# Two up matrices side by side on TensorE's column halves in the 64-slot expert steps of a two-layer mixture-of-experts block

## The chip, the cores and the metric

One core of one Trainium2 chip runs the whole program. The metric is device time in microseconds (us), the median of several runs. The engines are PE (TensorE matmul), ACT (ScalarE), DVE (VectorE), POOL (GpSimd) and SP (SyncE, which issues most transfers).

## What is computed

A block of two layers over 256 tokens of width 1024 (with 256 context tokens beside them in the first layer). Each layer has a group of sequence mixers and then a mixture of 16 experts, of which each token takes two. All inputs are float32. Cut to the part that the change touches:

```python
def moe(h, w_router, b_router, w1, w3, w2):
    logits = (h @ w_router).astype(F32) + b_router.astype(F32)
    ...
    for e in range(N_EXPERTS):
        he = jax.nn.silu(h @ w1[e]) * (h @ w3[e])
        out = out + gate[..., e:e + 1].astype(h.dtype) * (he @ w2[e])
    return out

def reference(x, c, ctx, ...):
    for l in range(DEPTH):
        ...
        x = x + gt2 * moe(h2, router_w, router_b, moe_w1[l], moe_w3[l], moe_w2[l])
    return rms_norm(x, final_norm_g)
```

`w1[e]` and `w3[e]` (the up matrices) are 1024 x 512, `w2[e]` (the down matrix) is 512 x 1024.

## The kernel before

Tokens are sorted to experts: each expert `e` of layer `l` has `SLOT[l][e]` slots (rows of tokens), and what doesn't fit runs in a loop of extra passes between experts 1 and 2 (`extras`). `moe` (L1923) walks the experts; each is a generator, `expert32` (L2163) or `expert`, whose stages are interleaved with those of the expert before, so that the up products of `e` stand around the down product of `e - 1`. In layer 1 all experts run in `expert32`, fourteen of them with 64 slots, one with 128 (e = 4) and one with 96 (e = 8). In layer 0 only the seven with 64 slots do; the others split each weight into a high and a low part for three matmuls. These 21 steps with 64 slots are the subject.

A step's weights are six loads of 1 MB ("raw"): j = 0, 1 are the two row halves of w1 (four blocks of 128 rows each), j = 2, 3 those of w3, j = 4, 5 the two column halves of w2. The table `USE` (L43) sets the order in which they are fetched: (e,0), then the down halves of e - 1, then (e,1), (e,2), (e,3). SP issues them into a ring of buffers, 10 in layer 0 and 12 in layer 1, at most three under way at once (`FLIGHT`); a load waits until PE has read the ring's buffer.

`expert32` with 64 slots (G = 2) uses half of PE's columns for one matmul, because the stationary operand has 64 columns. `tile_position` gives even row blocks the lower and odd row blocks the upper half of the columns:

```python
            a = k % G
            kw = dict(tile_position=(0, a * m)) if G > 1 else {}
            ... nc.tensor.matmul(ps[a * m:a * m + m], lhsT=lhsT, rhs=next(ws), start=k < G, stop=k >= n - G, ...)
```

A product therefore leaves as two partial sums, in partitions 0 to 63 and 64 to 127 of a PSUM bank, to be joined:

- Up: `p1` (w1) and `p3` (w3) are two banks of sixteen matmuls together. ACT copies `p1` and DVE copies `p3` to SBUF (tiles `al`). Eight matmuls against the constant `fold`, two identity blocks stacked, add the halves and transpose at once. ACT's Silu and a DVE product make `h` (tile `ah`), which is the stationary operand of the down product.
- Down: for each of the two column halves four matmuls into a bank; ACT copies the upper partitions (tile `s`), DVE adds the lower ones, and ACT scales by the gate (ACTIVATE, `y` or `yf`). When both halves are done, POOL issues a scatter with addition of 64 rows of 4 KB into the accumulator `ybd` in HBM (`add_rows`, L2153).
- The last expert (e = 15) is not scattered. `combine` joins its rows to the accumulated ones through a one-hot matrix on PE, after `ybd` has been read back by SP and multiplied on POOL.

PE, ACT, DVE, POOL and SP each run their instructions in order. A scheduler fixes each order at build time. Two stages that recur below: `xg` is the gathered token rows of an expert, transposed on PE (`tp`) and copied by ACT (`ah`); `sc`, `mm` and `tp` are the names of PSUM banks for up products, down products and transposes. In the profile nearly every operation carries one line number, L385 (L395 in the changed program), that of a recording helper, so its rows are read by these names.

Of the kernel before, what the change touches and what calls it, by code (L numbers as in the profile page):

```python
# [19 lines left out]
P = 128  # L20
# [20 lines left out]

STAT = 2
USE = [(0, j) for j in range(4)]  # L43
for _e in range(1, NE):
    _p = [(_e, 0), (_e - 1, 4), (_e - 1, 5)]
    USE += (_p if _e != STAT else _p[1:] + _p[:1]) + [(_e, j) for j in range(1, 4)]
USE += [(NE - 1, 4), (NE - 1, 5)]
# [19 lines left out]
TILE = [np.cumsum([0] + [-(-n // P) for n in SLOT[l]]).tolist() for l in range(L)]  # L67
NXMAX = 16
# [323 lines left out]
class Kern:  # L392
# [114 lines left out]
    def pump(self):  # L507
        I = self.I
        while self.lp < len(self.items):
# [9 lines left out]
            if k[0] == "x" and k[2] < BUFS[f"R{k[1]}"]["raw2"]:  # L519
                src = I["wmoe"][self.wpos(k[1], *USE[k[2]])]  # L520
                t = self.rp.tile([P, 2048], F32, tag="raw2", name=self.nm("raw"), bufs=BUFS[f"R{k[1]}"]["raw2"])
            else:
# [3 lines left out]
                src = {"x": lambda: I["wmoe"][self.wpos(k[1], *USE[k[2]])], "w": lambda: I["win"][k[1], k[2]], "o": lambda: I["wout"][k[1], k[2]],  # L526
# [102 lines left out]
    def setup(self):  # L629
# [17 lines left out]
        self.fold = cp.tile([P, HALF], F32, name="fold")  # L647
        nc.vector.tensor_tensor(self.fold, self.ident[:, 0:HALF], self.ident[:, HALF:P], op=ALU.add)
# [1058 lines left out]
    def route(self, l, NT):  # L1707
# [139 lines left out]
        nc.gpsimd.dma_start(tab, self.slv(l)[:, 0:TILE[l][NE]])  # L1847
        yield
# [17 lines left out]
    def first_slots(self, l):  # L1866
# [7 lines left out]
        for tag, n, dt in (("src", STAT, I32), ("cnt", 16, F32), ("key", 16, F32), ("cap", 16, F32), ("big", nd * nd, F32), ("rke", 16, F32),  # L1874
                           ("sel", nd * nd, BF16), ("ext", 16, F32), ("inc", 16, F32), ("exc", 16, F32), ("nx", 1, I32),
                           ("at", 16, F32), ("ov", 16 * NT, F32), ("u", 16 * NT, F32), ("w", 16 * NT, F32),
                           ("XT", 4 * NT, F32), ("q", 2 * NT, F32), ("r", 2 * NT, F32), ("ri", 2 * NT, I32), ("tab", 2 * TILE[l][NE], I32)):
# [45 lines left out]
    def moe(self, l, route):  # L1923
# [12 lines left out]
        def begin(e):  # L1936
            if self.whole(l, e):
                gens[e] = self.expert32(l, source(e), (xg.pop(e), *sl[e]), SLOT[l][e], last=e == NE - 1)
# [9 lines left out]
        for e in range(NE):  # L1948
            for n, t in zip(both(e), range(TILE[l][e], TILE[l][e + 1])):
                sl[n] = self.slot_of(self.rt["tab"][:, t])  # L1950
        begin(0)
        next(gens[0])
        for e in range(NE):
            if e == STAT:

                while len(self.pre) < AHEAD2[l]:
                    m, j = USE[self.wi]
# [15 lines left out]
            if e == NE - 1:  # L1973
                while self.wi < len(USE):
                    self.pre.append(self.fetch(source(USE[self.wi][0])(USE[self.wi][1])))
# [187 lines left out]
    def expert32(self, l, wsrc, tile, m, last=False):  # L2163
# [9 lines left out]
        G = 2 if m == HALF else 1  # L2173

        def weights():
            for j in range(6):
                raw = self.load(wsrc(j))
                for k in range(4):
                    yield raw[:, k * 512:(k + 1) * 512]

        ws = weights()

        def mm(ps, lhsT, k, n):
            a = k % G
            kw = dict(tile_position=(0, a * m)) if G > 1 else {}
            self.last_mm = nc.tensor.matmul(ps[a * m:a * m + m], lhsT=lhsT, rhs=next(ws), start=k < G, stop=k >= n - G,
                                            skip_group_check=True, **kw)
# [11 lines left out]
        p1, p3 = self.pssc(), self.pssc()  # L2199
        for w, ps in enumerate((p1, p3)):  # L2200
            for k in range(KB):
                mm(ps, x[k], k, KB)
                if (w, k) in ((0, 1), (0, 3), (1, 3)):
                    yield
        s1 = self.act("al", F32)
        if G > 1:
            s3 = self.act("al", F32)
            nc.scalar.copy(s1, p1)
            nc.vector.tensor_copy(s3, p3)
        else:  # L2210
            nc.scalar.activation(s1[:m], p1[:m], AF.Silu)
# [3 lines left out]
        if G > 1:  # L2215
            for j, s in enumerate((s1, s3)):
                for k in range(4):
                    o = (4 * j + k) * m
# [155 lines left out]
```

## Time and profile before

| | |
|---|---|
| median of 3 runs | 1288.04 us (1285.62 to 1288.15) |
| the profiled execution's own time | 1281.23 us |
| its span | 1279.6 us |
| PE busy | 1128.9 us, 88% |
| DVE, ACT, POOL busy | 722.7, 531.5, 162.9 us |
| mean granted clock of PE | 0.945 of full speed |

The span runs from the first to the last instruction of one execution on the core; the run's time lies 1.6 us above it. The profiled execution is 0.53% faster than the median. In the span the experts of layer 0 stand at about 444 to 710 us, those of layer 1 at 985 to 1257 us, with the loop of extra passes at 1014 to 1026 us; the rest is mixers, routing and the final norm.

### The profile page before, as it was taken

The page shows a single profiled execution, that of the slowest core. Times are in us where ns is not written, and L with a number is a line of the kernel's source. Part 1 is how long each engine was busy: PE and PEld are TensorE (multiplying, and loading weights), DVE is VectorE, ACT ScalarE, POOL GpSimd, SP SyncE. Part 2 cuts the span into 40 slices and gives each one's busy share as a digit, 9 for nine tenths or more (in the row PEclk, how much of TensorE's full clock was granted, in tenths as well). Part 3 has the DMA queues.
Part 4 walks back from the last instruction along what each step waited for, and adds up shares of the span by engine and source line. Part 5 has one row for each costly group of instructions (what it writes and reads, how often), then busy time and mean ns, then how long its engine had stood idle before and what let it go on. Part 6 is the DMA issues. An engine that isn't in the chain of part 4 may idle for free. (4 is left out here: it accounts for less than half of the span.)

```text
span 1279.6 us, 16887 instructions
## 1 busy us (share of the span) xinstructions
PE 1128.9 (88%) x5789; PEld 714.7 (56%) x5789; DVE 722.7 (56%) x1824; ACT 531.5 (42%) x877; POOL 162.9 (13%) x204
## 2 busy tenths in 40 slices
PE   4999999997977699999998799998893699998885
PEld 2677677765866467655444277684771344533332
DVE  6396579788588554455444659599975110101115
ACT  5232642675316554555434452563940212222222
POOL 0100200100004210211100100200202111111102
PEclk9999999997987899999999899999995999998997
DMA  8773753443917798899994744554468989999961
GB/s 304 255 250 113 257 206 112 168 176 125 393 67 276 252 341 321 310 367 380 387 394 163 283 180 143 177 203 162 147 234 320 372 333 390 376 391 389 412 248 67
DMA packets 62010, 334.06 MB, mean 261 GB/s; under 512 B 12217, under 2 KB 13657, under 8 KB 27104
## 3 DMA queue, kind: packets, MB, share of 16 engines
q1 hardware_dynamic: 51840, 313.44, 64.5%
q0 software_dynamic: 10080, 19.50, 5.9%
q8 instruction: 47, 0.77, 0.2%
q14 instruction: 43, 0.35, 0.1%
HBM read 317.51 MB, written 19.15 MB: 263 GB/s over the span
## 5 line engine op out<-in xcount | busy, mean ns | idle before, releaser
L385 DVE TENSOR_TENSOR lo<-raw,hi 128x1024 fp32r<-128x1024 f32 x172 | 206.6, 1220 | 90.2 <-ACT hi L385 78.1
L385 PE MATMUL sc<-raw,ah 128*64 128x512 f32 (+3 forms) x750 | 214.1, 628 | 14.8 <-SPq L2042 11.7
L385 ACT CAST hi<-raw 128x1024 fp32r<-128x1024 f32 x169 | 172.3, 1047 | 123.2 <-PE sc L385 58.2
L385 PEld LDWEIGHTS sc<-raw,ah 128*64 128x64 f32 (+3 forms) x750 | 63.0, 146 | 115.2 <-issue 100.6
L385 PE MATMUL mm<-hi,ah 128*128 128x512 f32 (+3 forms) x264 | 108.7, 413 | 5.0 <-ACT hi L385 4.6
L385 PE MATMUL mm<-lo,ah 128*128 128x512 f32 (+3 forms) x264 | 106.5, 403 | 1.8 <-DVE lo L385 1.6
L385 PE MATMUL mm<-hi,al 128*128 128x512 f32 (+3 forms) x264 | 105.4, 401 | 0.3 <-DVE al L385 0.3
L385 PE MATMUL mm<-raw,ah 128*64 128x512 f32 (+3 forms) x378 | 98.3, 592 | 2.5 <-DVE rel L385 1.9
L385 DVE COPY al<-sc 128x512 f32<-128x512 f32 x21 | 14.5, 691 | 149.3 <-PE sc L385 129.6
L385 PE MATMUL mm<-ah,hi 128*128 128x512 f32 (+1 forms) x224 | 86.9, 393 | 0.8 <-DVE ah L385 0.8
L385 PE MATMUL sc<-hi,ah 128*128 128x512 f32 (+3 forms) x176 | 74.2, 423 | 14.2 <-issue 10.5
L385 PE MATMUL mm<-ah,lo 128*128 128x512 f32 (+1 forms) x224 | 83.0, 371 | 0.9 <-DVE lo L385 0.9
L385 PE MATMUL mm<-al,hi 128*128 128x512 f32 (+1 forms) x224 | 82.9, 370 | 0.0
L385 PE MATMUL ad<-raw,cT 128*32 128x256 f32 (+1 forms) x512 | 67.3, 526 | 10.8 <-DMA raw<-in_wada_dram 9.1
L385 DVE TENSOR_TENSOR s<-s,mm 64x512 f32<-64x512 f32 (+1 forms) x43 | 29.2, 678 | 81.5 <-ACT s L385 81.5
L385 PE MATMUL sc<-lo,ah 128*128 128x512 f32 (+3 forms) x176 | 72.7, 413 | 1.7 <-DVE lo L385 1.6
L385 PE MATMUL sc<-hi,al 128*128 128x512 f32 (+3 forms) x176 | 72.1, 409 | 1.8 <-DVE al L385 1.8
L385 PEld LDWEIGHTS mm<-hi,ah 128*128 128x128 f32 (+3 forms) x264 | 49.2, 187 | 28.3 <-ACT hi L385 6.5
L385 PEld LDWEIGHTS mm<-raw,ah 128*64 128x64 f32 (+3 forms) x378 | 32.6, 142 | 57.7 <-issue 48.5
L385 PEld LDWEIGHTS tp<-fold,al 128*128 128x128 f32 x336 | 40.5, 191 | 38.6 <-ACT al L385 15.6
L385 PE MATMUL tp<-fold,al 128*128 128x64 f32 x336 | 43.8, 278 | 15.8 <-ACT al L385 8.6
L385 PEld LDWEIGHTS mm<-lo,ah 128*128 128x128 f32 (+3 forms) x264 | 49.4, 187 | 14.6 <-DVE lo L385 4.6
(433 smaller groups left out, 1952.8 us busy)
## 6 DMA issues: line engine op xcount, KB each, us to landing
raw<-in_wmoe_dram SPq DMA_DIRECT2D x192, 1024.0 KB, 7.9
raw<-in_wada_dram SPq DMA_DIRECT2D x32, 1024.0 KB, 5.1
raw<-in_win_dram SPq DMA_DIRECT2D x24, 1024.0 KB, 6.2
raw<-in_wad_dram SPq DMA_DIRECT2D x16, 1024.0 KB, 4.9
raw<-in_wout_dram SPq DMA_DIRECT2D x8, 1024.0 KB, 5.0
x<-in_tok_dram SPq DMA_DIRECT2D x8, 512.0 KB, 7.4
raw<-ybd SPq DMA_DIRECT2D x6, 512.0 KB, 4.7
slot<-yf SPq DMA_DIRECT2D x36, 64.0 KB, 2.8
```

What stands on the lines that cost most here:

```text
L385: r = f(*a, **k)
```

## The change

In a step with 64 slots the column halves now take different matrices, not different row blocks. For each of the eight row blocks two matmuls run with the same stationary operand: w1 on the lower, w3 on the upper half, into one bank. All rows of a product are summed in place, so nothing is left to be joined. One ACT copy brings the bank to SBUF, four plain transposes of 128x128 follow, and Silu and product read the two halves of each transposed block. The eight down matmuls likewise put the two column halves of w2 side by side in one bank, one ACTIVATE scales all 128 partitions, and the scatter writes 128 pieces of 2 KB (row and half) instead of 64 of 4 KB.

Raws are now read in pairs, (0,2) and (1,3), then (4,5); `USE` becomes a table for each layer, in which both raws of the first pair come before the down halves of e - 1. For the scatter's 128 rows and gates the routing adds a table `tab2` (two small loads on POOL's queue a layer) and `row2` (one POOL operation a layer). In the last expert the upper half of the down bank is copied by ACT and the lower is read in place. Steps with other numbers of slots keep their instructions. In layer 0's seven steps the four transposes stand behind other matmuls of the neighbouring expert in four cases, and right behind the step's own up matmuls in three. At the start of layer 1 and in its mixers a few small loads and weight matmuls move by some places.

```diff
+def _use(l):
+    out = []
+    for e in range(NE):
+        js = [0, 2, 1, 3] if SLOT[l][e] == HALF else [0, 1, 2, 3]
+        n = 2 if SLOT[l][e] == HALF else 1
+        down = [(e - 1, 4), (e - 1, 5)] if e else []
+        up = [(e, j) for j in js]
+        out += down + up if e == STAT else up[:n] + down + up[n:]
+    return out + [(NE - 1, 4), (NE - 1, 5)]
...
-        self.fold = cp.tile([P, HALF], F32, name="fold")
-        nc.vector.tensor_tensor(self.fold, self.ident[:, 0:HALF], self.ident[:, HALF:P], op=ALU.add)
+        self.half = cp.tile([P, 1], F32, name="half")
+        nc.vector.reduce_sum(self.half, self.ident[:, HALF:], axis=AX.X)
...
+        tab2 = self.rt["tab2"] = f([P, TILE[l][NE], 2], "tab2", I32)
+        for h in range(2):
+            nc.gpsimd.dma_start(tab2[h * HALF:(h + 1) * HALF], self.slv(l)[0:HALF, 0:TILE[l][NE]])
...
+            if e == 0:
+                nc.gpsimd.tensor_scalar(self.row2, self.rt["tab2"][:, :, 0], 2.0, self.half, op0=ALU.mult, op1=ALU.add)
...
+        if m == HALF:
+            self.nc.gpsimd.indirect_dma_start(out=self.ybd[l].rearrange("r (h c) -> (r h) c", h=2), out_offset=bass.IndirectOffsetOnAxis(ap=rows, axis=0),
+                                              in_=y[:, 0:512], in_offset=None, bounds_check=2 * self.rt["NT"] * P - 1, oob_is_err=False,
+                                              compute_op=ALU.add)
+            return
...
-        p1, p3 = self.pssc(), self.pssc()
-        for w, ps in enumerate((p1, p3)):
-            for k in range(KB):
-                mm(ps, x[k], k, KB)
-                if (w, k) in ((0, 1), (0, 3), (1, 3)):
-                    yield
...
         if G > 1:
-            s3 = self.act("al", F32)
-            nc.scalar.copy(s1, p1)
-            nc.vector.tensor_copy(s3, p3)
+            ps = self.pssc()
+            ws = chain.from_iterable(weights(c, 2 + c) for c in range(2))
+            for k in range(KB):
+                for a in range(2):
+                    mm(ps, x[k], next(ws), a, k == 0, k == KB - 1)
+                if k in (1, 3, 5):
+                    yield
+            nc.scalar.copy(s1, ps)
...
-            for j, s in enumerate((s1, s3)):
-                for k in range(4):
-                    o = (4 * j + k) * m
-                    nc.tensor.matmul(pt[:, o:o + m], lhsT=s[:, k * P:(k + 1) * P], rhs=self.fold, start=True, stop=True)
+            for k in range(4):
+                nc.tensor.transpose(pt[:, k * P:(k + 1) * P], s1[:, k * P:(k + 1) * P], self.ident)
...
+        if G > 1:
+            ps = self.psmm()
+            ws = weights(4, 5)
+            for k in range(4):
+                for a in range(2):
+                    mm(ps, h[:, k * m:(k + 1) * m], next(ws), a, k == 0, k == 3)
+            if not last:
+                nc.scalar.activation(y[:, 0:512], ps, AF.Copy, scale=half[1])
+                self.add_rows(l, y, half[0], m)
+                return
+            t = self.act("al", F32)[:m]
+            nc.scalar.copy(t, ps[m:2 * m])
```

The orders move at three places that matter below. First PE in a late step of layer 1, before: `ah_10268` feeds the down product of e - 1, `al_10347` and `al_10348` are the copies of `p1` and `p3`, `xg` belongs to e + 2.

```order
L385 MATMUL sc_10262<-raw_10264,ah_10247 64x512 x4
L385 MATMUL mm_10283<-raw_10284,ah_10268 64x512 x4
L385 MATMUL mm_10294<-raw_10295,ah_10268 64x512 x4
L385 MATMUL sc_10262<-raw_10308,ah_10247 64x512 x4
L385 MATMUL tp_10361<-fold,al_10347 128x64 x4
L385 MATMUL tp_10422<-cst,xg_8996 128x64 x4
L385 MATMUL sc_10263<-raw_10314,ah_10247 64x512 x4
L385 MATMUL tp_10422<-cst,xg_8996 128x64 x4
L385 MATMUL sc_10263<-raw_10341,ah_10247 64x512 x4
L385 MATMUL tp_10361<-fold,al_10348 128x64 x4
```

And the same place in the changed program, from the end of a step's up product on (`al_10205` is the one copy; the matmuls on `raw_2180` and `raw_2181` alternate, and the next expert's down matmuls on `raw_10303` and `raw_10305` do):

```order
L395 MATMUL sc_10206<-raw_10247,ah_10195 64x512
L395 MATMUL sc_10206<-raw_10245,ah_10195 64x512
L395 MATMUL sc_10206<-raw_10247,ah_10195 64x512
L395 MATMUL tp_10290<-cst,al_10205 128x128 x3
L395 MATMUL sc_10280<-raw_2180_10281,ah_10272 64x512
L395 MATMUL tp_10290<-cst,al_10205 128x128
L395 MATMUL tp_10337<-cst,xg_8903 128x64 x8
L395 MATMUL sc_10280<-raw_2181_10283,ah_10272 64x512
L395 MATMUL sc_10280<-raw_2180_10281,ah_10272 64x512
...
L395 MATMUL sc_10280<-raw_2181_10283,ah_10272 64x512
L395 MATMUL mm_10302<-raw_10303,ah_10289 64x512
L395 MATMUL mm_10302<-raw_10305,ah_10289 64x512
```

The two sets of folds, one ahead of the second and one behind the last up matmuls, have become one set of transposes behind the last up matmul, and one matmul of the next expert's up product has slipped in among them; the down matmuls keep their place among the up matmuls.

Second, ACT over such a step, before:

```order
L385 COPY s_2250_10474<-mm_10467 64x512
L385 ACTIVATE yf_6832<-s_2250_10474,rtab_9095 64x512
L385 COPY s_2253_10485<-mm_10478 64x512
L385 ACTIVATE yf_6832<-s_2253_10485,rtab_9095 64x512
L385 COPY al_10531<-sc_10446 128x512
L385 ACTIVATE al_10551<-tp_10542 128x256
L385 COPY ah_10612<-tp_10603 128x512
```

and changed:

```order
L395 ACTIVATE yf_6737<-mm_10228,rtab_1966_9004 128x512
L395 COPY al_10205<-sc_10206 128x512
L395 ACTIVATE al_10295<-tp_10290 128x256
L395 COPY ah_10346<-tp_10337 128x512
...
L395 ACTIVATE yf_6737<-mm_10376,rtab_1966_9004 128x512
L395 COPY al_10353<-sc_10354 128x512
```

Four operations on the down product ahead of the copy of the up bank have become one; the last two rows are the same pair a step later, with no transposed token rows (`ah`) left to copy.

Third, DVE at the end of the program, before:

```order
L385 COPY al_10696<-sc_10625 128x512
L385 TENSOR_TENSOR ah_10699<-al_10709,tp_10700 128x256
L385 TENSOR_SCALAR rel_10713<-rtab_9095 64x1 x2
L385 TENSOR_SCALAR ah_10712<-iota_b,rel_10713 64x128 x2
L385 TENSOR_TENSOR s_2307_10724<-s_2307_10724,mm_10719 64x512
L385 SCALAR_TENSOR_TENSOR s_2308_10727<-s_2307_10724,rtab_9095,raw_10688 64x512
L385 TENSOR_TENSOR raw_10718<-s_2308_10727,raw_10718 64x512
L385 TENSOR_TENSOR s_2310_10736<-s_2310_10736,mm_10731 64x512
L385 SCALAR_TENSOR_TENSOR s_2311_10739<-s_2310_10736,rtab_9095,raw_10688 64x512
L385 TENSOR_TENSOR raw_10718<-s_2311_10739,raw_10718 64x512
```

and changed:

```order
L395 TENSOR_TENSOR ah_10413<-al_10419,tp_10414 128x256
L395 TENSOR_SCALAR rel_10423<-rtab_9002 64x1 x2
L395 TENSOR_SCALAR ah_10422<-iota_b,rel_10423 64x128 x2
L395 SCALAR_TENSOR_TENSOR s_2215_10440<-mm_10429,rtab_9002,raw_10405 64x512
L395 SCALAR_TENSOR_TENSOR s_2216_10444<-al_10438,rtab_9002,raw_10405 64x512
L395 TENSOR_TENSOR raw_10428<-s_2215_10440,raw_10428 64x512
L395 TENSOR_TENSOR raw_10428<-s_2216_10444,raw_10428 64x512
```

The copy of `p3` and the two additions to `s` are gone, and the two halves of the last product stand side by side, not one after the other.

## Rows read from the trace of the kernel before

All times are us of the span. A row of a group of instructions names line, engine, operation, output<-input with tile shapes, and the count of records.

**Rows 1.** The page, part 1: busy us (share of span) and instructions.

```profile
PE 1128.9 (88%) x5789; PEld 714.7 (56%) x5789; DVE 722.7 (56%) x1824; ACT 531.5 (42%) x877; POOL 162.9 (13%) x204
```

**Rows 2.** Busy time by stretch, all engines, then granted clock, DMA share, GB/s.

```profile
core 0: us, PE busy (x) PEld busy (x) DVE busy (x) ACT busy (x) POOL busy (x), PEclk, DMA share, GB/s
...
1056.00:1106.00 50.00, 50.00 (x218) 23.12 (x216) 5.78 (x10) 11.82 (x20) 7.36 (x6) 1.00 1.01 383
...
1156.00:1206.00 50.00, 43.65 (x216) 17.65 (x214) 7.42 (x12) 11.83 (x21) 6.17 (x5) 0.93 1.01 399
1206.00:1257.00 51.00, 43.73 (x207) 17.16 (x204) 11.18 (x16) 11.46 (x20) 8.67 (x5) 0.93 0.64 255
1257.00:1279.60 22.60, 9.72 (x16) 3.76 (x16) 11.12 (x27) 5.83 (x13) 2.75 (x3) 0.68 0.13 47
```

**Rows 3.** Waits of 1026 to 1257 us: total us, times, longest.

```profile
PE tp L385 <- ACT al L385: 8.6, 7, 1.3
...
PE tp L385 <- DVE al L385: 5.6, 7, 0.8
...
PEld sc L385 <- DMA raw<-in_wmoe_dram: 0.9, 2, 0.6
```

**Rows 4.** Waits of SP's DMA queue, 1026 to 1240 us.

```profile
SPq L385 <- DMA raw<-in_wmoe_dram: 147.1, 70, 4.7
SPq L385 <- PE sc L385: 6.3, 9, 1.5
```

**Rows 5.** Loads of expert weights, 1056-1260 us: ns min/median/max, starts.

```profile
L385 SPq DMA_DIRECT2D raw<-in_wmoe_dram x62: 332/333/348, 1056.7 to 1226.5; - x62
...
DMA to landing us min/median/max: 6.5/7.9/12.1
```

**Rows 6.** Timeline of PE, 1155-1174 us: start, length, group [idle before].

```profile
1160.87 1.10 PE L385 MATMUL tp<-fold,al 128*128 128x64 f32 x8 [1.32 <-ACT al L385]
...
1162.29 3.33 PE L385 MATMUL sc<-raw,ah 128*64 128x512 f32 x8
...
1168.90 1.10 PE L385 MATMUL tp<-fold,al 128*128 128x64 f32 x8 [0.79 <-DVE al L385]
```

**Rows 7.** Timeline of PE, 1238 to 1258 us.

```profile
1253.28 3.65 PE L385 MATMUL mm<-raw,ah 128*64 128x512 f32 x16 [0.93 <-DVE rel L385]
```

**Rows 8.** Groups by shape, 1026 to 1257 us: busy, mean ns, idle before.

```profile
L385 PE MATMUL sc<-raw,ah 128*64 128x512 f32 x384 | 101.6, 645 | 11.7 <-SPq L2042 11.7
...
L385 PE MATMUL tp<-fold,al 128*128 128x64 f32 x192 | 25.5, 279 | 14.2 <-ACT al L385 8.6 <-DVE al L385 5.6
...
L385 ACT COPY al<-sc 128x512 f32<-128x512 f32 x12 | 7.0, 585 | 17.7 <-PE sc L385 17.3
...
L385 POOL TENSOR_TENSOR raw<-raw,raw 128x1024 f32<-128x1024 f32 x2 | 4.7, 2350 | 5.8 <-PE tp L385 5.8
...
L385 ACT ACTIVATE yf<-mm,rtab 128x512 f32<-128x512 f32 x2 | 1.4, 687 | 6.8 <-PE mm L385 6.8
...
L385 PE MATMUL tp<-cst,xg 128*128 128x128 f32 x8 | 1.1, 280 | 0.0
```

**Rows 9.** Groups by shape in layer 0's experts, 444 to 710 us.

```profile
L385 PE MATMUL tp<-fold,al 128*128 128x64 f32 x112 | 14.1, 275 | 1.6 <-DVE al L385 1.6
```

**Rows 10.** Waits of 444 to 710 us.

```profile
PE sc L385 <- ACT hi L385: 3.7, 2, 1.9
```

**Rows 11.** Loads of expert weights, 640 to 712 us.

```profile
L385 SPq DMA_DIRECT2D raw<-in_wmoe_dram x14: 332/333/333, 639.9 to 678.5; - x14
```

**Rows 12.** Timeline of PE, 630 to 710 us.

```profile
705.79 3.65 PE L385 MATMUL mm<-raw,ah 128*64 128x512 f32 x16 [0.93 <-DVE rel L385]
```

**Rows 13.** The accumulator ybd from 1240 us to the end: its DMAs.

```profile
L385 POOL DMA_INDIRECT ybd<-yf,rtab x1: 1408/1408/1408, 1245.4 to 1245.4; - x1
...
DMA to landing us min/median/max: 3.4/3.5/4.8
```

**Rows 14.** DMA queues, 1026 to 1240 us: packets, MB, share of 16 engines.

```profile
q0 software_dynamic: 2112, 3.40, 6.7%
```

More of the change, by code (lines that the diff above doesn't have):

```diff
@@ L42 @@
 STAT = 2
[L43 to L47, printed above, removed]
 RESERVE = (8, 8)
@@ L67 @@
 TILE = [np.cumsum([0] + [-(-n // P) for n in SLOT[l]]).tolist() for l in range(L)]
+def _use(l):
[7 more added lines that the diff above has]
+    return out + [(NE - 1, 4), (NE - 1, 5)]
+USE = [_use(l) for l in range(L)]
 NXMAX = 16
@@ L1937, in begin @@
             if self.whole(l, e):
-                gens[e] = self.expert32(l, source(e), (xg.pop(e), *sl[e]), SLOT[l][e], last=e == NE - 1)
+                t = TILE[l][e]
+                half = (self.row2[:, t:t + 1], self.slot_of(self.rt["tab2"][:, t])[1]) if SLOT[l][e] == HALF else None
+                gens[e] = self.expert32(l, source(e), (xg.pop(e), *sl[e]), SLOT[l][e], half, last=e == NE - 1)
             else:
@@ L1950, in moe @@
                 sl[n] = self.slot_of(self.rt["tab"][:, t])
+        self.row2 = self.sx([P, TILE[l][NE]], "rrow2", I32)
         begin(0)
@@ L2161, in whole, with expert32 @@
         return l == 1 or SLOT[l][e] <= HALF
-    def expert32(self, l, wsrc, tile, m, last=False):
+    def expert32(self, l, wsrc, tile, m, half=None, last=False):
         nc = self.nc
@@ L2172, in expert32, with weights, mm @@
         g, NT = gate[:m], self.rt["NT"]
[L2173 to L2177, printed above, removed]
-                for k in range(4):
+        G = 2 if half else 1
+        def weights(*js):
+            raws = [self.load(wsrc(j)) for j in js]
+            for k in range(4):
+                for raw in raws:
                     yield raw[:, k * 512:(k + 1) * 512]
-        ws = weights()
-        def mm(ps, lhsT, k, n):
-            a = k % G
+        def mm(ps, lhsT, w, a, first, end):
             kw = dict(tile_position=(0, a * m)) if G > 1 else {}
-            self.last_mm = nc.tensor.matmul(ps[a * m:a * m + m], lhsT=lhsT, rhs=next(ws), start=k < G, stop=k >= n - G,
-                                            skip_group_check=True, **kw)
+            self.last_mm = nc.tensor.matmul(ps[a * m:a * m + m], lhsT=lhsT, rhs=w, start=first, stop=end, skip_group_check=True, **kw)
         x = []
@@ L2239, in expert32 @@
         y = None if last else self.yring()
+        if G > 1:
+            ps = self.psmm()
+            ws = weights(4, 5)
+            for k in range(4):
+                for a in range(2):
[6 more added lines that the diff above has]
+            nc.scalar.copy(t, ps[m:2 * m])
+        else:
+            ws = chain(weights(4), weights(5))
         for n in range(2):
-            py = self.psmm()
-            for k in range(4):
-                mm(py, h[:, k * m:(k + 1) * m], k, 4)
             c = slice(n * 512, n * 512 + 512)
-            ps = py[:m]
             if G > 1:
-                t = self.pg("s1", 512)[:m]
-                nc.scalar.copy(t, py[m:2 * m])
-                nc.vector.tensor_tensor(t, t, ps, op=ALU.add)
-                ps = t
+                ps = t if n else ps[:m]
+            else:
+                ps = self.psmm()
+                for k in range(4):
+                    mm(ps, h[:, k * m:(k + 1) * m], next(ws), 0, k == 0, k == 3)
+                ps = ps[:m]
             if last and l == 1:
```

26 lines of the change are left out of this document (17 added, 9 removed).

## The prediction

> **What bounds the kernel now.** I read the page first: PE is busy for 1128.9 of 1279.6 us, far ahead of any other engine [rows 1]. That is an average, so the table of stretches comes next. Between 1056 and 1106 us PE is busy for all 50.00 us, and the DMA engines are full as well (share 1.01). Between 1156 and 1206 us the DMA share is still 1.01, but PE has fallen to 43.65 us and its granted clock to 0.93. After 1206 us the DMA share drops to 0.64 while PE goes on [rows 2]. So two things run neck and neck in the second layer's experts, and the question is which is ahead. The waits say it: PE's weight loads wait 0.9 us in all for expert weights, while the transposes and folds wait 8.6 us for ACT and 5.6 us for DVE [rows 3]. The queue that fetches weights waits almost only for its own transfers (147.1 us) and 6.3 us for a buffer that PE holds [rows 4]. Hence PE sets the end of the layer, and the weights run at their own pace, a little ahead of it. How far ahead: the last of 62 loads is issued at 1226.5 us and lands some 7.9 us later [rows 5], at 1234.4; PE finishes the last down product at 1253.28 + 3.65 = 1256.93 us [rows 7]. The cushion at the end is 22.5 us. This is the number that caps the gain. The pace is (1226.5 - 1056.7) / 61 = 2.78 us a load, 16.7 us for the six of an expert.
>
> **Layer 1, PE's own work (12 steps after the mid-layer barrier).** Removed: the folds, 192 records, 25.5 us busy, 2.13 us a step [rows 8]. Added: four 128x128 transposes a step; eight of that shape took 1.1 us [rows 8], so 0.55 us a step. The weight matmuls keep their number and shape (384 and 192 records), since both column halves still work side by side. That is 25.5 - 12 x 0.55 = 18.9 us less.
>
> Second, the stalls. In the seven late steps PE waits 1.32 us for ACT ahead of the first four folds and 0.79 us for DVE ahead of the second four [rows 6], 14.2 us in all [rows 3]. ACT's wait is longer than its copy (585 ns [rows 8]) because that copy stands in ACT's queue behind two copies and two scalings of the previous down product. The changed order has one ACTIVATE there, and one PSUM bank to copy. I take one stall a step, as long as DVE's now, which has one copy and nothing in its way: 0.79 us, 5.5 for seven. The gain is 8.7 us. Were the ACTIVATE (687 ns [rows 8]) still in the way each time, it would be 4.8 us less. In the early steps the transposes stand behind the next expert's matmuls, as the folds did, and cost no wait.
>
> Third, the clock. Behind the 1.32 us gap eight records take 3.33 us [rows 6] instead of about 1.83, half of the sixteen in [rows 7]; the stretch has a mean granted clock of 0.93 [rows 2]. Such dips cost up to 1.5 us in perhaps four steps, so 0 to 6 us may come back; I take none. PE's work by itself would thus end 27.6 us earlier (22.8 to 33.6).
>
> **Layer 1, the cap.** 27.6 us is more than the cushion. The last two loads are a pair that PE reads alternately, so the last eight instructions (3.65 us [rows 7]) cannot finish before both landed: 1234.4 + 3.65 = 1238 us, against 1256.9. I take **19 us** from this layer. PE then ends in waits for weights, which is what is late next. The stream itself could run earlier by the 6.3 us it now loses to PE [rows 4] (gain 25), or be slower (below).
>
> Layer 1's first two experts lie before the barrier; their folds too go, 2 x 1.6 us, but other work ends there: 1 us (0 to 3.2).
>
> **Layer 0 (seven steps).** 112 fold records cost 14.1 us [rows 9], seven sets of transposes 3.9: 10.2 us less. Of those sets three stand right behind their own matmuls and wait 0.79 us each, 2.4 in all, against 1.6 us of idle before the folds now [rows 9]: 0.8 us more. ACT's copies and scalings of the down product hold back its casts for the next expert, for which PE waits 3.7 us [rows 10]; I take 2 us of that back (0 to 3.7). Here the cushion is no limit: the last load is issued at 678.5 us [rows 11], lands by about 686, and PE ends at 709.4 [rows 12], 23 us later. 10.2 - 0.8 + 2 is 11.4, taken as **11 us** (7 to 14).
>
> **The end of the program.** The last product's halves now become ready together and need no DVE addition, about 1.4 us less. But the accumulated rows must be read back after the previous expert's scatter: that was issued at 1245.4 us, and scatter landing (3.4), load (4.8) and two POOL products (2 x 2.35 [rows 8]) follow [rows 13], 12.9 us, to 1258.3. With PE caught up, only four loads (11.1 us) and not 14 us lie between the two last down products, and the scatter may land among weight loads, up to 4.5 us later. I take 1 us of loss (gain of 2 to loss of 5). A queue's order of small loads at the layer boundary moves too, on SP; I bound that by one short landing, 3.5 us [rows 13], either way, and take 0, because PE there waits for other chains.
>
> **New work.** Two small table loads and one POOL multiply a layer are off PE's path in stretches where POOL is busy 6 to 9 us of 50 [rows 2]: 1 us of loss taken; from 0 to one landing of 3.5 us a layer. The scatter has 128 pieces of 2 KB instead of 64 of 4 KB. It uses the same DMA engines as the weights; all indirect traffic takes 6.7% of them over 214 us, 14.3 us [rows 14]. If pieces cost by bytes, nothing changes; if by count, the scatters' part of it doubles, at most +14.3 us on a stream that is now the cap. I take 0, nearest to the byte count, and keep +14 as a rival. The Trainium skill, "DMA: Bandwidth & Descriptors", Specifications, puts the smallest transfer at line rate at 512 B; by that the 2 KB pieces cost nothing extra and the sum stays. No row before shows an accumulating piece of 2 KB.
>
> **Sum.** 19 + 1 + 11 - 1 - 1 = 29 us. The profiled execution took 1281.23 us, so 1252.2; the median shown is 1288.04, 0.53% above it, so about **1259 us** for the median.
>
> **The rivals.**
> - *The stream moves too.* Buffers come free sooner and loads use the 6.3 us: 25 instead of 19, and with the layer's other upper ends (2 from the first experts, 1 from layer 0) 1259 - 6 - 3 = 1250. For it: the 9 waits on PE [rows 4]. Against it: the DMA share is 1.01 anyway [rows 2].
> - *The scatter lengthens the stream.* +14 us: 1273. For it: the share 1.01; against it, nothing that prices a piece.
> - *Layer 1 is bound by the stream already* and only layer 0 gains: 1278. Against it: 22.5 us of cushion [rows 5, 7] and 0.9 us of waits [rows 3].
> - *Slower: PE waits in little pieces and loses its clock.* Once it has caught up, PE waits for every pair of loads. After such a gap the trace shows 3.33 us for eight records [rows 6], and the quiet end stands at a clock of 0.68 [rows 2]. If the low level (1.2 GHz of 2.4) lasts through whole steps, the 48 records take 6 x 3.33 = 20 us, with transposes at half speed (1.1) and the stall (0.8) 21.9 a step, 5.2 more than the stream's 16.7. It decides from six steps on: 6 x 5.2 eats the 29 us. With nine it is 1259 + 47 = 1306. Against it: with 2 us of stalls a step the mean clock still was 0.93 [rows 2], and waiting PE has slack. The Trainium skill, "TensorE: Matmul & The Clock Gate", HAM oscillation, describes a kernel that waits for each K tile's data and starts every tile at the low clock; by that rule this rival would come true. The trace agrees for single gaps only.
> - *The change does nothing*, because the folds' place is taken by other waits: 1288.
>
> **How the numbers follow.** Forecast 0.50, earlier stream 0.16, longer scatter 0.17, layer 0 alone 0.07, low clock 0.07, nothing 0.03. A measurement of this kernel can tell about 0.2% (2.6 us) from no change. Faster by more: 0.90; within it 0.03; slower 0.07. The range takes the first three cases with their costs: the low end is the earlier stream's 1250 and 6 us for a tail that gains and small loads that come earlier, 1244; the high end the longer scatter's 1273 and 2 us of new work, 1275.
>
> **What would show it.** Right: no fold records; 0.55 us of transposes a step; one stall of about 0.7 us in late steps; PE's waits for expert weights in layer 1 grow from 0.9 us to 10 us or more, and the last down product ends within 5 us of the last landing near 1234 us of the old clock (some 12 us earlier by layer 0's gain and the first experts'). Layer 0's experts end 11 us sooner. Wrong: the span from the last landing to PE's end stays above 10 us (PE still the bound), the pace of loads is longer than 16.7 us an expert (scatter), or groups of eight records at 3.3 us fill the late steps (clock).

## The result, and the profile after

The changed kernel took 1269.51 us (median of 4 runs, 1265.63 to 1275.28) against 1286.83 us; the ratio is 0.9867 with a 95% interval of 0.984 to 0.9895. Run again beside the experiments it took 1264.61 us against 1287.04 us, a ratio of 0.9841 (0.9816 to 0.9866). These ratios, and those below, are not quotients of the two medians, from which they differ by up to 0.2%; gains over the kernel before are given by the ratio. So the change is worth 17 to 20 us (22 by the second pair of medians), where 29 were forecast: the sign was right and the time lies in the stated range, but the forecast gain was 1.4 to 1.7 times the measured one.

Of the changed kernel, the page's PE row, and the row that names where the chain of work that ended last spent its time:

```profile
PE 1108.8 (88%) x5537; PEld 684.7 (54%) x5537; DVE 681.3 (54%) x1761; ACT 496.8 (39%) x818; POOL 169.2 (13%) x210
...
DMA 10%; PE 8%; DVE 0%; issue 0%; POOL 0%; ACT 0%; DVEq 0%; SPq 0%; POOLq 0%; ACTq 0%
```

PE is busy 20 us less than in [rows 1]. What is new is the second row: the chain now runs through weight transfers. The same row of the kernel before has none:

```profile
PE 15%; DVE 2%; ACT 2%; issue 0%; DVEq 0%; ACTq 0%
```

The same table of stretches as [rows 2], of the changed kernel, with a stretch of layer 0 ahead:

```profile
core 0: us, PE busy (x) PEld busy (x) DVE busy (x) ACT busy (x) POOL busy (x), PEclk, DMA share, GB/s
...
600.00:650.00 50.00, 44.31 (x180) 23.38 (x179) 20.92 (x22) 20.05 (x27) 5.32 (x5) 0.93 1.02 391
...
1056.00:1106.00 50.00, 50.00 (x208) 19.15 (x206) 1.53 (x3) 8.98 (x16) 8.64 (x7) 1.00 1.02 386
...
1156.00:1206.00 50.00, 44.62 (x202) 15.04 (x198) 1.31 (x4) 7.69 (x14) 7.61 (x6) 1.00 1.01 403
1206.00:1240.00 34.00, 28.02 (x121) 8.70 (x118) 1.78 (x7) 4.05 (x8) 3.12 (x2) 1.00 0.95 381
```

In layer 1 the clock no longer falls (1.00 where [rows 2] had 0.93), and the DMA share stays at 0.95 to the end of the experts, where it was 0.64. Layer 0 went the other way: the kernel before has a clock of 1.00 between 600 and 650 us, as the same view of it shows:

```profile
600.00:650.00 50.00, 47.37 (x228) 25.33 (x224) 23.75 (x27) 25.61 (x36) 6.75 (x5) 1.00 1.01 396
```

The waits that answer to [rows 3], of the changed kernel between 1026 and 1240 us:

```profile
PEld sc L395 <- DMA raw<-in_wmoe_dram: 10.7, 9, 2.2
...
PE sc L395 <- DMA raw<-in_wmoe_dram: 5.2, 4, 1.3
PEld mm L395 <- DMA raw<-in_wmoe_dram: 4.4, 4, 1.7
...
PE tp L395 <- ACT al L395: 4.1, 6, 0.7
```

PE's weight loads for up products (`PEld sc`) waited 0.9 us for weights and now wait 10.7. The wait for the copy is one of 0.7 us a step. The stream answers to [rows 5] almost unmoved:

```profile
L395 SPq DMA_DIRECT2D raw<-in_wmoe_dram x63: 332/333/342, 1057.3 to 1227.8; - x63
```

That is (1227.8 - 1057.3) / 62 = 2.75 us a load against 2.78, and the last issue is 1.3 us later than before. SP's queue waits for its own transfers as before ([rows 4]), hardly for PE (1026 to 1240 us):

```profile
SPq L395 <- DMA raw<-in_wmoe_dram: 148.4, 69, 4.3
...
SPq L395 <- PE sc L395: 7.2, 8, 3.2
```

PE's late steps, from the timeline of the changed kernel:

```profile
1214.77 3.65 PE L395 MATMUL sc<-raw,ah 128*64 128x512 f32 x14 [1.33 <-DMA raw<-in_wmoe_dram]
...
1236.14 3.65 PE L395 MATMUL mm<-raw,ah 128*64 128x512 f32 x16 [0.93 <-DVE rel L395]
...
1243.38 2.00 PE L395 MATMUL sc<-raw,cst 128*128 128x512 f32 x3 [3.58 <-POOL raw L395]
```

The last down product ends at 1236.14 + 3.65 = 1239.79 us, 4 us after the last landing (1227.8 + 7.9), not 22.5. The last row is new as well: PE waits 3.58 us for the read-back rows.

To see where the time went I cut each profile into stages at PE's first matmul behind the two loops of extra passes, at the last expert's down product and at the first matmuls between them; the lengths come from the timelines. They repeat within 3 us for one code, mostly within 1, while the start of the first stage moves by up to 8 us from one execution to the next (so whole spans compare badly, and stages well):

```
                     layer 0's   mixers   layer 1's      layer 1,    end of
                     experts              experts 0, 1   from e = 2  program
before               265.2       274.2    42.5           230.9       22.6
before again         264.7       276.6    42.6           230.9       22.7
change               262.8       272.7    43.2           213.1       24.2
change again         264.6       272.7    44.8           213.3       23.8
layer 1 alone        265.1       279.3    44.2           213.5       22.7
layer 0 alone        262.7       273.6    43.2           228.5       21.1
casts ahead          263.8       275.3    44.2           213.1       22.3
change, no w3        262.8       272.9    42.6           190.8       21.2
before, no w3        264.8       276.7    42.6           207.6       23.2
DVE products         265.7       274.7    44.5           214.2       23.0
scale on DVE         258.9       274.3    43.8           213.4       23.9
identity matmul      256.5       273.8    44.6           214.0       21.2
both                 255.2       273.6    43.1           214.8       25.1
```

Layer 1 gave 17.8 us, against 19 forecast. Layer 0's experts gave 0.1 to 2.4 us by the two profiles of either kernel, against 11; over all runs, the five executions with the change's layer 0 stand at 262.7 to 265.7 us and the four with the old one at 264.7 to 265.2. Experts 0 and 1 lost 0.6 to 2.3 us where a gain of 1 was expected, and the end lost 1.1 to 1.6 us where 1 was. The mixers, to which the forecast gave nothing, took 272.7 to 275.3 us in the nine executions with a changed layer 0 and 274.2 to 279.3 us in the four without, some 3 us less on the mean.

### The profile page after: what moved, and what is told of

It reads as the page before. It is cut to its first block, busy times and chain, and to the rows that moved or that the text cites. A ratio compares the mean times of both kernels' runs of the same rounds, so it can differ in the third digit from the quotient of the medians.

```text
span 1264.0 us, 16213 instructions
## 1 busy us (share of the span) xinstructions
PE 1108.8 (88%) x5537; PEld 684.7 (54%) x5537; DVE 681.3 (54%) x1761; ACT 496.8 (39%) x818; POOL 169.2 (13%) x210
## 5 line engine op out<-in xcount | busy, mean ns | idle before, releaser
L395 PE MATMUL sc<-raw,ah 128*64 128x512 f32 (+3 forms) x750 | 216.2, 612 | 20.8 <-SPq L2062 14.9
L395 DVE TENSOR_TENSOR ah<-al,tp 128x256 f32<-128x256 f32 x21 | 8.8, 419 | 230.0 <-ACT al L395 197.6
L395 PE MATMUL mm<-raw,ah 128*64 128x512 f32 (+3 forms) x378 | 105.1, 595 | 3.4 <-DVE rel L395 1.9
L395 PEld LDWEIGHTS mm<-hi,al 128*128 128x128 f32 (+3 forms) x264 | 49.8, 189 | 11.4 <-DVE al L395 0.8
L395 PEld LDWEIGHTS mm<-ah,hi 128*128 128x128 f32 x224 | 42.0, 190 | 22.1 <-issue 9.7
L395 PEld LDWEIGHTS sc<-hi,ah 128*128 128x128 f32 (+3 forms) x176 | 33.0, 187 | 31.0 <-issue 14.4
```

The source lines that it names most:

```text
L395: r = f(*a, **k)
```

## The experiments

### One layer at a time

The kernel with the changed steps, tables and order only in the layers named in a constant, and the old `expert32` and `USE` elsewhere:

```diff
+NEWL = (1,)
...
+    if l not in NEWL:
+        ...
-                half = (...) if SLOT[l][e] == HALF else None
+                half = (...) if SLOT[l][e] == HALF and l in NEWL else None
```

> Layer 0's seven steps as before (folds, row blocks), layer 1's fourteen steps changed. Theory A (the gain of layer 1 is real and capped by the weight stream, layer 0 gave nearly nothing): 14 to 17 us faster than before, as much as the whole change. The prediction's own sum: 19 us from layer 1 less 1 at the end and 0.5 of new work, 17 to 19 us. Theory B (both layers share the measured gain in the proportion 19 to 11): about 11 us.

Measured: 0.989 (0.9866 to 0.9915), 14 us faster than 1287.04.

> Layer 0's seven steps changed, layer 1's as before. Theory A: 0 to 4 us faster than before. The prediction's own sum: 11 us faster. Theory B: about 6 us.

Measured with `NEWL = (0,)`: 0.9947 (0.9927 to 0.9967), 7 us faster.

> The change itself, beside the others on one chip: 14 to 20 us faster than before. In its profile layer 0's experts end within 4 us of before's if theory A holds, and 8 to 11 us earlier if the first profile only had a late start.

Measured: 0.9841 (0.9816 to 0.9866), 20 us faster. The two parts add up to the whole. Layer 0's experts ended at 708.3 us, 1.1 us earlier than in the first profile of the kernel before, within theory A's 4 us. Layer 1 gave at least theory A's lower end. Layer 0 gave more than theory A allowed and less than the forecast, nearest to theory B; but its stage in that execution's profile is only 2 us shorter, and 2.4 us lie in layer 1, whose code is that of before. What layer 0 is worth is thus between 2 and 9 us by these runs, and under the forecast by either measure.

> The kernel before once more, for a second profile, since the first was of one of its faster executions. If that profile is typical, layer 0's experts take 265 us from the loop of extra passes to the last down product and layer 1's 231 us, within 1 us; if not, the 4 to 6 us between that execution and the median lie in one of them, or in the stretches between.

One execution took 1291.41 us. The stages are those of the first profile to 0.5 us, except for 2.4 us in the mixers; 7.3 us lie ahead of 451 us, where the change does nothing. The first profile's faster time says nothing about the experts.

### Is layer 1 now bound by its weights

Both kernels, with the loads of w3 left out for the 64-slot experts from 2 on in layer 1 (the table loses these entries, and the raws of w1 are read twice):

```diff
+    return [(e, j) for e, j in out if not (short(l, e) and j in (2, 3))]
...
-            raws = [self.load(wsrc(j)) for j in js]
+            raws = [self.load(wsrc(j)) for j in js if not (sh and j in (2, 3))]
+            raws = (raws * 2)[:len(js)]
```

> The change without the loads of w3 in layer 1's 64-slot experts after the barrier: w1's rows are used for both matrices, so PE's work is the same and the stream a third shorter. Theory A (after the change layer 1 ends with the weight stream): PE's waits for weights (6 us in the changed kernel's late steps) vanish, and with them the late read-back of the accumulated rows; 6 to 11 us faster than the change, 24 to 30 us faster than before. Rival (PE still is the bound): within 2 us of the change.

Measured: 0.9653 (0.9622 to 0.9685) against before, 44 us faster, and 22 us less in layer 1's stage. The waits for weights are nearly gone, and PE keeps one step of 11.8 us to the end. From the waits between 1028 and 1220 us and from the timeline of PE:

```profile
PEld sc L400 <- DMA raw<-in_wmoe_dram: 2.0, 5, 0.8
...
PE tp L400 <- ACT al L400: 0.7, 1, 0.7
```

```profile
1168.30 0.65 PE L400 MATMUL tp<-cst,al 128*128 128x128 f32 x4
...
1180.12 0.66 PE L400 MATMUL tp<-cst,al 128*128 128x128 f32 x4
```

SP's queue, which waited for transfers before the cut, now waits for PE (1028 to 1220 us):

```profile
SPq L400 <- PE sc L400: 66.1, 27, 3.8
SPq L400 <- PE mm L400: 37.1, 13, 3.1
...
SPq L400 <- DMA raw<-in_wmoe_dram: 19.6, 19, 2.2
```

So with the full loads the stream is the bound of the changed kernel, and without a third of them PE is. The stage is 22 us shorter, twice what was expected, because PE did not only lose gaps: its idle time in the stage fell from 11.3 to 1.7 us, and the same 832 records took 12.8 us less. PE's last six steps took 12.7 to 16.0 us with the full stream. The order differs as well: with the full stream the late steps have their transposes right behind their own up matmuls and single matmuls of two products by turns, and with the cut they keep the order of the early ones, in which the changed kernel itself takes 11.83 us a step (1086.17 to 1098.00 us). What late weights cost and what that order costs, the run does not part.

> The same cut in the kernel before: w1's rows used for both matrices in layer 1's 64-slot experts after the barrier. Theory A (before, PE was the bound and the stream 22 us ahead): no change, 0 to 3 us faster. Rival (the stream bound both kernels): 10 us faster or more.

Measured: 0.9868 (0.9835 to 0.9902), 17 us faster, and 23.3 us less in the stage. By the letter the rival wins. The trace shows another difference: with fewer loads the scheduler, which plans with the loads' times, wrote another order for the late steps. All sixteen fold records stand together behind the next expert's matmuls. From the timeline of PE:

```profile
1210.86 2.00 PE L391 MATMUL tp<-fold,al 128*128 128x64 f32 x16
...
1224.17 2.00 PE L391 MATMUL tp<-fold,al 128*128 128x64 f32 x16
```

There is no wait ahead of them (in [rows 6] there is), and PE's step is 13.31 us, where the kernel before has 14.2 to 17.5 us in its last six steps. PE's idle time in the stage fell from 15.2 to 1.0 us, and the matmuls and folds between took 9 us less, as the clock stayed up (0.99 for the stage, 0.96 before) and the order was another. So this run doesn't test the bound of the kernel before, as it changed two things. What it does give is PE's own step by both codes, without waits: 13.3 and 11.8 us. The early steps of the two kernels with all loads have the same lengths, 13.30 (1086.24 to 1099.54 us) and 11.83 us. The difference of 1.5 us is the fold's price less that of the transposes; the prediction had 2.13 - 0.55 = 1.58. It also shows that the late steps' stalls and low clock cost the kernel before about 23 us, and that they go with the order that was written for the full stream.

### The end of the program

```diff
-                nc.gpsimd.tensor_tensor(y, y, self.g2r[0], op=ALU.mult)
+                for h in range(2):
+                    c = slice(h * 512, h * 512 + 512)
+                    nc.vector.tensor_tensor(y[:, c], y[:, c], self.g2r[0][:, c], op=ALU.mult)
```

> The change with the product of the read-back rows and the layer's gate on DVE in four pieces of 512 columns, not on POOL in two of 1024 (2.35 us each). Theory: PE waits 3.58 us for the first POOL product at the end and a second one follows; on DVE the first piece takes 0.7 us and the additions beside it no longer run beside POOL (2.74 and 1.7 us each there against 0.74 and 0.7 without): 1 to 3 us faster than the change, 19 to 23 us faster than before. Rival (DVE's own queue is the bound of the end): no gain.

Measured: 0.9825 (0.9793 to 0.9856), 1265.09 us, not to be told from the change (1264.61). The end is 23.0 us long, 1 us less than in the change. In DVE's timeline the four products took 2.48 us together, and the additions ran at 0.7 us each, as expected, but the products stand behind four of these operations in DVE's queue, and PE waited 4.09 us. The rival holds: DVE's queue took POOL's place.

### Layer 0: why the folds' time came back

In its seven steps PE lost 13.1 us of folds and gained 3.7 us of transposes, 9.4 us, near the forecast 10.2 (where two records overlap, the time is counted once, for the earlier, so 13.1 stands where [rows 9] has 14.1). Against that stand waits and a lower clock. The waits of the changed kernel between 444 and 712 us, to compare with [rows 10]:

```profile
PE sc L395 <- ACT hi L395: 3.4, 2, 1.7
PE mm L395 <- ACT hi L395: 2.6, 2, 1.5
PE sc L395 <- DVE lo L395: 2.6, 4, 0.8
...
PE tp L395 <- ACT al L395: 2.1, 3, 0.7
PE mm L395 <- DVE lo L395: 1.6, 2, 0.8
```

Before, PE had waited 3.7 us for casts ahead of up products and hardly ahead of down products; the second is the row of the same view of the kernel before:

```profile
PE mm L385 <- ACT hi L385: 0.5, 1, 0.5
```

The rise from 0.5 to 2.6 us comes from an order in ACT's queue: there a cast stands behind a copy of transposed token rows which itself waited for PE, as ACT's timeline of the changed kernel shows, and after it PE's:

```profile
612.89 0.48 ACT L395 CAST ah<-tp 128x384 fp32r<-128x384 f32 x1 [3.58 <-PE tp L395]
613.27 1.99 ACT L395 CAST hi<-raw 128x1024 fp32r<-128x1024 f32 x2
```

```profile
614.37 0.47 PE L395 MATMUL mm<-hi,ah 128*96 128x512 f32 x1 [1.18 <-ACT hi L395]
```

PE's idle time in the stage rose from 9.9 to 13.3 us. The rest of the matmuls, the same in number and shape, took 245.7 us where they had taken 242.2 (both sums over the stage's records). The next view is the timeline of PE in the changed kernel:

```profile
638.50 0.48 PE L395 MATMUL sc<-hi,ah 128*96 128x512 f32 x1 [1.71 <-ACT hi L395]
639.76 0.48 PE L395 MATMUL sc<-lo,ah 128*96 128x512 f32 x1 [0.78 <-DVE lo L395]
...
640.40 0.63 PE L395 MATMUL sc<-hi,ah 128*96 128x512 f32 x1
640.83 0.63 PE L395 MATMUL sc<-lo,ah 128*96 128x512 f32 x1
```

Behind the two waits the records start 0.43 us apart, not 0.23, up to 643.39 us: the clock at its lower level, 1.2 of 2.4 GHz. At the same place the kernel before had waits as long, and no such records follow, as its timeline of PE shows:

```profile
636.97 0.48 PE L385 MATMUL sc<-hi,ah 128*96 128x512 f32 x1 [1.85 <-ACT hi L385]
638.23 0.47 PE L385 MATMUL sc<-lo,ah 128*96 128x512 f32 x1 [0.78 <-DVE lo L385]
...
639.00 0.40 PE L385 MATMUL sc<-lo,ah 128*96 128x512 f32 x1
```

> The change, and in layer 0 the first half of each split expert's second raw is fetched and cast before the down product of the expert before is issued, so that ACT has the cast ahead of the scaling that waits for PE. Theory C (in layer 0 the folds' time comes back as waits for ACT's casts, which stand in ACT's queue behind the one ACTIVATE on the down bank, with DVE's low part and a lower clock behind them): two of three waits of 1.7 + 0.8 us go, and with them the clock's dip; 4 to 8 us faster than the change, 21 to 25 us faster than before. Rival D (layer 0 is held by its weight loads, or the difference was only this execution's late start): as the change, within 2 us.

The edit fetches both halves of w1 ahead of the down halves and makes the generator of a split expert take one more half raw ahead of its yield:

```diff
+                    if look and (w, c, hf) == (0, 0, 1):
+                        ws = chain([next(ws), next(ws)], ws)
```

Measured: 0.9826 (0.9807 to 0.9845), 22 us faster than before and within the interval of the change. In its profile the waits of 1.71 and 0.78 us stand one half raw later and are as long: the cast after the next is behind the scaling again. By its time rival D would win, but the run says nothing on theory C, as its edit did not remove the wait.

```diff
-                nc.scalar.activation(y[:, 0:512], ps, AF.Copy, scale=half[1])
+                if l == 0:
+                    nc.vector.tensor_scalar(y[:, 0:512], ps, half[1], None, op0=ALU.mult)
+                else:
+                    nc.scalar.activation(y[:, 0:512], ps, AF.Copy, scale=half[1])
```

> The change with layer 0's six scalings of the down bank on DVE, not ACT, so that nothing which waits for the down product stands ahead of ACT's casts for the next expert. Theory C (the folds' time in layer 0 comes back as waits behind ACT's queue and the lower clock after them): PE's waits of 1.7 us for a cast vanish from layer 0, the waits for DVE's low part grow from 0.8 to at most 1.9 us; layer 0's stage from the loop of extra passes to its end, 262.7 to 265.7 us in the profiles of the change, becomes 259 to 262 us; 2 to 5 us faster than the change in all. Rival E (it is the transposes and the copy ahead of them that let the clock fall): the stage stays at 262 to 265 us, with the clock between 600 and 650 us at 0.93 as now.

Measured: 0.9799 (0.9772 to 0.9826). Layer 0's stage is 258.9 us, 4 to 6 us less than the change's. Its waits in the same stretch:

```profile
PE sc L395 <- DVE lo L395: 4.2, 4, 1.6
PE mm L395 <- ACT hi L395: 2.7, 2, 1.5
```

The waits for ACT's casts ahead of up products are gone and those for DVE have grown from 2.6 to 4.2 us, both as theory C says. Those ahead of down products stay at 2.7 us, so the scaling is not their cause. The clock of the stretch that rival E names is neither its 0.93 nor full:

```profile
600.00:650.00 50.00, 45.22 (x192) 24.14 (x190) 23.02 (x24) 19.15 (x25) 8.19 (x5) 0.97 1.02 392
```

As medians, 1263.64 and 1264.61 us, the two are not told apart; the ratios to before are 0.9799 and 0.9841, with intervals that overlap.

```diff
-                nc.tensor.transpose(pt[:, k * P:(k + 1) * P], s1[:, k * P:(k + 1) * P], self.ident)
+                nc.tensor.matmul(pt[:, k * P:(k + 1) * P], lhsT=s1[:, k * P:(k + 1) * P], rhs=self.ident, start=True, stop=True)
```

> The change with the four transposes of a step done as plain matmuls against the identity (the same values; 8 records for 4, about 0.55 us more a step, 11 us over 21 steps if nothing hides it). Theory C: the stretch of 600 to 650 us in layer 0 keeps its granted clock of 0.93, and the stage gets 2 to 4 us longer, to 266 to 269 us; layer 1 changes by less than 2 us, since the stream bounds it. Rival E: the clock of that stretch goes back to 1.00 as in the kernel before, which gives back 3 us, so the stage stays within 1 us.

Measured: 0.976 (0.9736 to 0.9785), 1258.04 us: more work on PE, and 6 us faster than the change, which was run beside the earlier experiments on another chip; the intervals of the two ratios to the kernel before do not overlap. Layer 0's stage is 256.5 us, 6 to 8 us shorter than the change's. The stretch's row and the timeline of PE at the place that was shown above:

```profile
600.00:650.00 50.00, 46.03 (x217) 24.57 (x215) 21.71 (x24) 21.87 (x31) 7.11 (x5) 1.00 1.02 393
```

```profile
634.01 0.47 PE L395 MATMUL sc<-hi,ah 128*96 128x512 f32 x1 [1.75 <-ACT hi L395]
635.27 0.47 PE L395 MATMUL sc<-lo,ah 128*96 128x512 f32 x1 [0.79 <-DVE lo L395]
...
636.04 0.40 PE L395 MATMUL sc<-lo,ah 128*96 128x512 f32 x1
```

The waits are there, as long as before, and the clock stays at 1.00, as rival E says; the stage is 5 us or more below what either theory gave. So these waits alone do not let the clock fall. But the edit changed more than the four records: the order of PE's rows is another. In the change the down product ahead of the waits is cut into 2 and 14 matmuls:

```profile
630.82 1.07 PE L395 MATMUL mm<-raw,ah 128*64 128x512 f32 x2
```

Here it stands in one piece:

```profile
628.61 3.65 PE L395 MATMUL mm<-raw,ah 128*64 128x512 f32 x16
```

A wait of 0.51 us that the change has ahead of it is gone too, and so is the wait of 1.18 us at 614 us with a fall of the clock behind it. On the other side, the run with the scalings on DVE keeps the change's four transposes and its waits of 0.71 and 0.51 us, has one wait for the two, and no slow records follow (PE's timeline of that run):

```profile
629.37 0.66 PE L395 MATMUL tp<-cst,al 128*128 128x128 f32 x4 [0.71 <-ACT al L395]
...
641.10 0.47 PE L395 MATMUL sc<-lo,ah 128*96 128x512 f32 x1 [1.58 <-DVE lo L395]
...
641.87 0.40 PE L395 MATMUL sc<-lo,ah 128*96 128x512 f32 x1
```

So the transposes alone do not let it fall either. The Trainium skill, "TensorE: Matmul & The Clock Gate", Part 4: PE-mode transpose, says that a transpose doesn't count as PE-busy in the way a matmul does. The higher clock here fits that, but no run shows it by itself, since none changed the transposes and kept the order.

How the 6 to 8 us come together can be counted. The added records cost 3.3 us. Idle time fell from 13.3 to 10.6 us. Summed over the stage's records, the matmuls other than folds and transposes of `al` took 238.8 us here, 245.7 and 247.5 in the two profiles of the change, 242.2 before. A part of that is the clock: behind the first 8 us of the stage, the time at the lower level, read in stretches of 1 us, is 3.4 us before, 10.2 and 13.6 us in the two profiles of the change, 6.8 us with the scalings on DVE and 3.4 us here. At half speed half of it is lost, so 3.4 to 5.1 us came back by the clock. The remaining 3.5 us go with the order. In the stage a run of 2 matmuls on raws took 1.00 us to the next record's start, a run of 6 took 1.86 us and one of 8 took 1.87, one of 14 took 3.58 and one of 16 the same. A run with an odd number of pairs thus costs about 0.45 us more than its share; the change has 16 such runs in the stage and this kernel has 8.

> The change with both edits: layer 0's scalings on DVE and the four transposes of a step as plain matmuls against the identity. If waits behind ACT's queue and the lower clock are two separate costs, layer 0's stage falls below either's alone (258.9 and 256.5 us) to 252 to 255 us, and the kernel is 1 to 4 us faster than with the identity matmuls alone, 31 to 35 us faster than before. If they are one cost (the clock falls because of those waits), the stage stays at 256 to 257 us.

Measured: 0.978 (0.9757 to 0.9803), 1256.52 us; 28 us faster than before, where 31 to 35 were expected; the stage is 255.2 us, 1.3 us below the identity matmuls alone. That is just above what two separate costs should give and just below what one should, so the run does not decide. PE's idle time in the stage fell from 10.6 to 8.7 us, but the time at the lower clock rose from 3.4 to 6.8 us, and the kernel's time can't be told from that of the run before. Both are faster than the change, and than the kernel before by 2.2 to 2.4%.

## Why the prediction was right or wrong

- **Layer 1, PE's own work**: right. 1.5 us a step by the steps that don't wait, forecast 1.58.
- **Layer 1, the stalls**: right as to form. Late steps have one wait of 0.68 us a step, forecast 0.79.
- **Layer 1, the cap**: right, and it set the result. The last landing hardly moved, PE's end moved to 4 us behind it, and the stage lost 17.8 us of 19 forecast. That the stream binds it is shown by the cut of its loads: SP's waits for its own transfers fell from 148.4 to 19.6 us and those for PE rose from 8.3 to 103.2; of the 22 us that the stage lost, a part is the order's. The rival of an earlier stream is out: its last issue is 1.3 us later. So is that of the longer scatter: the pace is 2.75 us a load with 128 pieces, so 2 KB pieces cost the stream nothing that shows.
- **Low clock in layer 1**: out; the clock there is 1.00 from 1056 us up to the end, though PE waits for loads, by up to 1.33 us at a time. The rule by which the prediction had this rival come true did not hold for waits of this length.
- **Experts 0 and 1**: the sign was wrong. PE is done 2.6 us earlier, but waits 14.9 us there, not 11.7. PE's wait ends on SP's queue, which has six weight loads there; in the change five of them wait for transfers (11.9 us), before four did (9.5 us) and one waited for a buffer that PE held. By these rows it was the stream that ended last, which the sum left out; no edit tested it.
- **Layer 0** is the step that failed: "10.2 - 0.8 + 2 is 11.4, taken as 11 us". The folds went (9.4 us). "I take 2 us of that back" was wrong: the waits for ACT's casts ahead of up products went from 3.7 to 3.4 us only, since the one scaling that is left waits for the down product in ACT's queue just as the four operations did. That is shown by its move to DVE, which took these waits away. Ahead of down products 2.1 us of new waits for casts came in (0.5 to 2.6), from an order in ACT's queue that the sum did not have. In all PE's idle time rose by 3.4 us where the sum took 1.2 off. And the clock was left out of layer 0's sum: there the rest of the matmuls took 3.5 to 5.3 us longer, and the time at the lower clock (3.4 us before, 10.2 and 13.6 us after) makes 3.4 to 5.1 us of that. 9.4 less 3.4 and less 3.5 to 5.3 leaves 0.7 to 2.5 us of the 11. Why the clock falls more often stays open: it fell less with one wait removed and less with plain matmuls in another order, and no run parts transposes, waits and order.
- **The end**: 1 us of loss taken, 1.1 to 1.6 us measured. The scatter that the read-back waits for landed 7.1 us after its issue, among weight loads, not 3.4, as was feared.
- **New work**: its 1 us of loss was argued from stretches in the experts, while the new loads stand in the routing; layer 1's lies in the mixers, which show no loss, and layer 0's ahead of the first stage, where it can't be read.
- What stays open: why layer 0 alone is 7 us faster by its median and 2 by its stage (the mixers behind it, some 3 us shorter with a changed layer 0, may be a part; what shortens them is not known), and what moves the first 450 us of the program by 8 us between executions.

## What to carry to other kernels

Ahead of an edit that speeds up the bounding engine, work out how far the next resource is behind at the end of that stage; here 22.5 us of cushion named the gain of layer 1 within 2 us. An in-order engine that evacuates another's result holds back all that stands behind it, however few operations are left, so count positions in its queue and not operations. A forecast by busy time needs a term for the granted clock in every stage with waits, also where the clock is full before the edit. Where transposes on TensorE stand among waits, the same values by plain matmuls against the identity are worth a try: here that kernel was 6 us faster, though by an order that came with the edit as much as by the clock. When an edit makes a scheduler write another order, compare the orders before giving the gain to the edit.

## What the runs showed of the hardware

- Four 128x128 transposes took 0.66 us and the same by eight matmul records 1.16 us, yet the stage with the dearer form was 6 to 8 us shorter, by 3.4 to 5.1 us of clock, 2.7 us of idle time and another order.
- 128 accumulating pieces of 2 KB loaded the DMA engines no more than 64 of 4 KB: 2.75 and 2.78 us a weight load beside them.
- Runs of matmuls on the two column halves took as long with an odd number of pairs as with one pair more: 1.86 us for 6 and 1.87 for 8, 3.58 us for 14 and for 16.
- With PE in waits for loads of up to 1.33 us at a time, the granted clock stayed at 1.00.
- Three DVE operations beside two POOL products took 2.74 and twice 1.72 us (the mean of two) at the end of the changed kernel, and 0.73 and twice 0.67 us where the products were on DVE.
